# A decoder layer on one core: the MLP's up projection by seven block products instead of eight, its down projection in a part of its own

## The chip, the cores and the metric
The program runs on one core of one Trainium2 chip. Five engines work side by side: PE (TensorE, matrix products into PSUM), DVE (VectorE), ACT (ScalarE), POOL (GpSimd) and SP, which here only issues DMA. The metric is the device time of one execution in microseconds, lower is better. A framework orders the instructions of each engine ahead of time and puts in the semaphore waits that the tiles' memory calls for.

## The reference, cut to what matters
One decoder layer on 1024 tokens of width 1024, in float32: three token mixers, their gated merge, an output projection, cross-attention over a memory of 256 rows, and a feed-forward part (width 2816) with a causal convolution over three tokens. `u` and `v` are the two halves of one up projection.

```python
def conv_gated_ffn(h, w_up, conv_w, conv_b, w_down):
    u, v = jnp.split(h @ w_up, 2, axis=-1)
    u = lax.conv_general_dilated(u, conv_w[:, None, :], window_strides=(1,),
                                 padding=[(CONV_W - 1, 0)],
                                 dimension_numbers=('NWC', 'WIO', 'NWC'),
                                 feature_group_count=D_FF) + conv_b
    return (jax.nn.silu(u) * v) @ w_down
...
        branches = jnp.stack([o_hg, o_da, o_rw], axis=2)
        gate = jax.nn.sigmoid((g_pre + b_gate[l]).astype(jnp.float32)).astype(x.dtype)
        merged = jnp.sum(gate * jnp.einsum('bsnc,ncd->bsnd', branches, w_branch[l]), axis=2)
        x = x + merged @ w_out[l]
        h = rms_norm(x, norm_xa_g[l])
        x = x + memory_cross_attention(h, rms_norm(mem, norm_mem_g[l]), xa_wq[l], xa_wkv[l], xa_wo[l])
        h = rms_norm(x, norm_ffn_g[l])
        x = x + conv_gated_ffn(h, ffn_w_up[l], ffn_conv_w[l], ffn_conv_b[l], ffn_w_down[l])
    return rms_norm(x, final_norm_g)
```

## The kernel before
Every product is made of three: both operands are split into a high part (a cast to fp32r on ACT) and a low part (the rest, subtracted on DVE or POOL), and PE adds high x high, high x low and low x high in PSUM. A weight is loaded by SP into `raw` (512 KB), split into `whi` and `wlo` by `wsplit` (L125-139), and used as the stationary operand, 128x128 at a time, against 512 tokens. `job` (L141-157) computes 128 output channels for 1024 tokens: 8 channel tiles x 2 token halves x 3 = 48 matmuls into the PSUM tile `ps_d`.

The program's stages are, in order: projections and mixers; the merge of the three branches (2, 1, 0), in which `branch` loads a branch's output `oraw`, splits it, and `merge` multiplies it by the branch's weight and gates it with `mth` (DVE L1170 or L1172, POOL L1173, the running sum `acc`); the trunk (output projection, scores and context, three passes of `tokmajor`, with the norm and the transposes of 128 tokens at a time behind the last column quarter); the feed-forward part. Merge 2 is a background stream that fills PE during the mixers and is emptied by `drain` after the loads of branch 1 have been placed.

`ffn` (L1231-1294) goes two channel tiles f at a time. For each f: 48 matmuls for u, the convolution (ACT L1248, L1250, DVE L1251, L1252, ACT L1253 for silu), 48 for v, their product (DVE L1257), its split (ACT L1259, POOL L1260) and the split of 128 rows of the down weight `wdr` (ACT L1265, POOL L1266). Then `down` adds the two tiles' share of the output: 16 groups of 6 matmuls into `ps_dn`, and each group is added to the residual `xr` by DVE (L1290), 11 times over in all. PE alternates between the two products to the end.

The order of the work within an engine is set by the framework's scheduler, which simulates the program; two instructions may be swapped only if no data or memory stands between them. SP issues its loads in its own order: a load that waits for a buffer holds up those behind it. Tiles with one tag in a pool share `bufs` buffers; a pool opened after another is closed takes the same memory, and its first writers wait for the last readers there.

## Time and profile before
| what | value |
|---|---|
| time, median of 3 runs | 2477.51 us (2473.56 to 2480.95) |
| the profiled execution | 2482.2 us, span 2480.3 us, mean granted clock 0.99 |
| instructions | 36628, of these 15488 matmul rows on PE |
| busy: PE, weight loads, DVE, ACT, POOL | 97%, 81%, 47%, 32%, 22% |
| DMA, mean over the span | 80 GB/s |

Matmuls are pipelined: a row gives the duration of one from its start to the modelled end (0.39 us), while the next starts 0.23 us later, so the steps between starts are what a matmul costs. The feed-forward part runs from about 1754 us to the end, the merge from about 1300 to 1440, the trunk between them. A row of a group gives busy time and mean duration; the idle time after the bar is that of the engine before those instructions.

### The profile page before, as it was taken

What the parts mean: (1) busy time and instruction counts of PE and PEld (TensorE: products, weight loads), DVE (VectorE), ACT (ScalarE), POOL (GpSimd) and SP (SyncE); (2) the same over time, 40 slices, a digit from 0 to 9 for tenths busy, and PEclk for the clock granted to TensorE, in tenths of its full rate; (3) what the DMA queues carried; (4) which work ended last, traced back from release to release, by engine and by line L of the source; (5) the groups of instructions that cost most, each with busy time, mean ns of one, the idle gap of its engine ahead of it and who ended that gap; (6) DMA issues with size and microseconds to landing.
All of it is one profiled execution on the core that took longest, in us unless ns stands there. A gap on an engine that the chain in (4) does not pass through costs nothing.

```text
span 2480.3 us, 36628 instructions
## 1 busy us (share of the span) xinstructions
PE 2413.2 (97%) x15488; PEld 2018.9 (81%) x15488; DVE 1161.6 (47%) x1911; ACT 790.9 (32%) x1163; POOL 552.1 (22%) x465
## 2 busy tenths in 40 slices
...
GB/s 299 232 153 128 81 57 94 56 94 40 95 66 65 59 48 35 52 43 52 43 64 205 183 118 57 89 69 35 77 50 36 51 43 43 51 52 51 51 34 68
DMA packets 78436, 199.65 MB, mean 80 GB/s; under 512 B 23616, under 2 KB 28352, under 8 KB 78272
## 3 DMA queue, kind: packets, MB, share of 16 engines
...
## 4 chain that ended last, share of the span: by engine, by line
PE 81%; DVE 9%; issue 3%; ACT 3%; DMA 2%; POOL 2%; SPq 0%; DVEq 0%; POOLq 0%; ACTq 0%
PE ps_d L152 16%; PE ps_d L150 16%; PE ps_d L154 16%; PE ps_dn L1273 10%; PE ps_tm L1089 3%; PE ps_tm L1090 3%; PE ps_tm L1091 3%; PE ps_l L937 1%; PE ps_c L274 1%; DVE tha L450 1%; DVE tmpa L448 1%; PE ps_Y L274 1%; PE ps_o L766 1%; PE ps_T L1135 1%; PE ps_qk L1051 1%
## 5 line engine op out<-in xcount | busy, mean ns | idle before, releaser
L135 ACT CAST whi<-raw 128x1024 fp32r<-128x1024 f32 (+1 forms) x198 | 196.3, 997 | 749.9 <-PE ps_d L152 554.3
L150 PE MATMUL ps_d<-hThi,whi 128*128 128x512 f32 x1056 | 427.5, 405 | 2.6 <-DVE Ktt L256 2.2
L152 PE MATMUL ps_d<-hTlo,whi 128*128 128x512 f32 x1056 | 425.9, 404 | 0.0
L154 PE MATMUL ps_d<-hThi,wlo 128*128 128x512 f32 x1056 | 425.2, 403 | 0.0
L138 POOL TENSOR_TENSOR wlo<-raw,whi 128x1024 fp32r<-128x1024 f32 (+1 forms) x67 | 149.7, 2234 | 731.8 <-ACT whi L135 685.0
L1290 DVE TENSOR_TENSOR xr<-ps_dn,xr 128x512 f32<-128x512 f32 x176 | 119.9, 688 | 344.8 <-PE ps_dn L1273 344.6
L152 PE MATMUL ps_d<-h3Tlo,whi 128*128 128x512 f32 x704 | 275.4, 391 | 0.0
L154 PE MATMUL ps_d<-h3Thi,wlo 128*128 128x512 f32 x704 | 275.3, 391 | 0.0
L150 PE MATMUL ps_d<-h3Thi,whi 128*128 128x512 f32 x704 | 275.1, 391 | 0.1
L1273 PE MATMUL ps_dn<-wdh,ffact 128*128 128x512 f32 x704 | 246.4, 396 | 0.1
L150 PEld LDWEIGHTS ps_d<-hThi,whi 128*128 128x128 f32 x1056 | 200.6, 190 | 45.4 <-issue 3.2
L152 PEld LDWEIGHTS ps_d<-hTlo,whi 128*128 128x128 f32 x1056 | 200.6, 190 | 43.1 <-issue 4.8
L154 PEld LDWEIGHTS ps_d<-hThi,wlo 128*128 128x128 f32 x1056 | 200.4, 190 | 43.1 <-issue 4.2
L138 DVE TENSOR_TENSOR wlo<-raw,whi 128x1024 fp32r<-128x1024 f32 (+1 forms) x131 | 169.4, 1300 | 90.8 <-ACT whi L135 90.7
L1273 PEld LDWEIGHTS ps_dn<-wdh,ffact 128*128 128x128 f32 x704 | 132.2, 188 | 31.3 <-DVE xr L1290 0.5
L152 PEld LDWEIGHTS ps_d<-h3Tlo,whi 128*128 128x128 f32 x704 | 132.2, 188 | 29.6 <-DVE h3Tlo L1139 0.4
L150 PEld LDWEIGHTS ps_d<-h3Thi,whi 128*128 128x128 f32 x704 | 132.0, 188 | 29.5 <-ACT h3Thi L1138 0.3
L154 PEld LDWEIGHTS ps_d<-h3Thi,wlo 128*128 128x128 f32 x704 | 132.2, 188 | 29.2 <-POOL wlo L138 0.2
L1273 PE MATMUL ps_dn<-wdl,ffact 128*128 128x512 f32 x352 | 138.4, 393 | 0.0
L1260 POOL TENSOR_TENSOR ffact<-y,ffact 128x1024 fp32r<-128x1024 f32 (+1 forms) x23 | 57.6, 2505 | 174.2 <-ACT ffact L1259 174.2
L1273 PEld LDWEIGHTS ps_dn<-wdl,ffact 128*128 128x128 f32 x352 | 66.0, 188 | 15.4
L740 DVE CUSTOM_DVE_ANT_0 a_p<-ps_s,a_bias 128x512 f32<-128x512 f32 (+3 forms) x96 | 51.8, 552 | 52.3 <-PE ps_s L738 46.7
...
## 6 DMA issues: line engine op xcount, KB each, us to landing
raw<-t_in SPq DMA_DIRECT2D x66, 512.0 KB, 3.7
raw<-t_up SPq DMA_DIRECT2D x44, 512.0 KB, 3.6
th_dram<-th SPq DMA_DIRECT2D x24, 512.0 KB, 2.9
mth<-th_dram SPq DMA_DIRECT2D x24, 512.0 KB, 3.8
wdr<-ffn_w_down SPq DMA_DIRECT2D x22, 512.0 KB, 3.5
raw<-t_kv SPq DMA_DIRECT2D x16, 512.0 KB, 4.9
raw<-qk_dram SPq DMA_DIRECT2D x16, 512.0 KB, 3.6
oraw<-o_dram SPq DMA_DIRECT2D x12, 512.0 KB, 4.7
```

Source lines behind the costliest of these rows:

```text
L135: nc.scalar.copy(out=hi, in_=raw)
L138: eng.tensor_tensor(out=lo, in0=raw, in1=hi.bitcast(F32), op=ALU.subtract)
L150: nc.tensor.matmul(o, lhsT=hi[:, k, :], rhs=xhi(k, h), start=(k == 0), stop=False)
L152: nc.tensor.matmul(o, lhsT=hi[:, k, :], rhs=xlo(k, h), start=False, stop=False)
L154: nc.tensor.matmul(o, lhsT=lo[:, k, :], rhs=xhi(k, h), start=False, stop=(k == nk - 1))
L740: V.tensor_tensor_reduce(out=p_[:, a:b], in0=ps[:, 0:b - a], in1=bias[:, 1024 - n + a:1024 - n + b], op0=ALU.add, op1=ALU.max, scale=1.0, ...
L1089: nc.tensor.matmul(o, lhsT=xh, rhs=hi[:, k % 4, :], start=(k == 0), stop=False)
L1090: nc.tensor.matmul(o, lhsT=xh, rhs=lo[:, k % 4, :], start=False, stop=False)
L1091: nc.tensor.matmul(o, lhsT=xl, rhs=hi[:, k % 4, :], start=False, stop=(k == NK - 1))
L1260: G.tensor_tensor(out=lo, in0=y[:, ts], in1=hi.bitcast(F32), op=ALU.subtract)
L1273: T.matmul(ps, lhsT=acts[f][a][:, P * i:P * i + P], rhs=wd[f][b][:, 512 * c:512 * c + 512], start=(f == 0 and n == 0), stop=(f == NG - 1 a ...
L1290: V.tensor_tensor(out=xr[i][:, cs], in0=ps, in1=xr[i][:, cs], op=ALU.add)
```

## The change
Three stages are rewritten, and the memory between them is laid out anew.

- Up projection (`left`, `prod`, `right`, `ffn_up`). For each f the weights of u and v (rows of blocks A1, A2) by two halves of the channels, and the normed input by two channel halves and two token halves (B11 to B22), form products of two by two blocks. Seven products of sums of blocks replace the eight: S1 = A21 + A22, S2 = S1 - A11, S3 = A11 - A21, S4 = A12 - S2; T1 = B12 - B11, T2 = B22 - T1, T3 = B22 - B12, T4 = B21 - T2. The sums S are made on POOL (128x512) for each f, each of the seven left operands is split into a form `wf` (ACT, then DVE and POOL in turn). The right operands are made once, in `right`, from raw transposed copies of the normed input (`h3r`, 128x2048). The products are added up in PSUM where two share a target, and else by DVE from PSUM. The first three f start with the products that need no T. The gated product y is stored to DRAM.
- Down projection (`ffn_down`) after all f: for each half of the tokens all 22 tiles of weights and of the stored y are loaded and split, and all eight PSUM banks sum over the 22 tiles; the last three f are held back so that the four token tiles end one after another. The residual is stored in DRAM by the trunk and loaded again.
- Trunk and merge: the context projection runs in two passes of four token tiles (`split=True`); activations lie in 15 buffers of 8 KB a partition instead of 6 of 16 KB; merge 2 is emptied and its pool closed before branch 1 is loaded.

```diff
     def halves(self, nm):
-        return [[self.actp.tile([P, NK, 512], F32R, tag="act", name=f"{nm}{p}{h}") for h in range(2)] for p in ("hi", "lo")]
+        return [[[self.quad(f"{nm}{p}{h}") for g in range(2)] for h in range(2)] for p in ("hi", "lo")]
+
+    def quad(self, nm, dt=F32R, shape=(P, 4, 512)):
+        return self.actp.tile(list(shape), dt, tag="act", name=nm)
...
         self.tokmajor(qk_dram, h2, soft, split=True)
...
+        def last(q, i, o):
+            xs = xr[i][:, 256 * q:256 * q + 256]
+            V.tensor_tensor(out=xs, in0=o, in1=xs, op=ALU.add)
+            if q < 3:
+                return
+            nc.sync.dma_start(out=x2_dram[i], in_=xr[i])
...
+                A.copy(out=raw[g, i // 4][:, :, ts], in_=p3)
+                if i < 4:
+                    hi, lo = (x[:, :, ts] for x in X[g])
+                    A.copy(out=hi, in_=p3)
+                    V.tensor_tensor(out=lo, in0=p3, in1=hi.bitcast(F32), op=ALU.subtract)
+
+        self.tokmajor(vo_dram, pT, last, split=True)
+        return X, raw
...
+    def left(self, r1, r2, which, sp):
...
+        sums = {"S1": ("A21", "A22", ALU.add), "S2": ("S1", "A11", ALU.subtract), "S3": ("A11", "A21", ALU.subtract),
+                "S4": ("A12", "S2", ALU.subtract)}
...
+                G.tensor_tensor(out=q[n], in0=a, in1=b, op=op)
...
+            f = self.wp.tile([P, 2, 4, P], F32R, tag=("whi", "wlo")[self.nform % 2], name="wf")
+            A.copy(out=f[:, 0], in_=x)
+            (V if self.nform % 2 else G).tensor_tensor(out=f[:, 1], in0=x, in1=f[:, 0].bitcast(F32), op=ALU.subtract)
+            yield f
+
+    def prod(self, ps, f, x, start, stop):
+        n = 0
+        for k in range(4):
+            for a, b in ((0, 0), (0, 1), (1, 0)):
+                self.nc.tensor.matmul(ps, lhsT=f[:, a, k, :], rhs=x[b][:, k, :], start=(start and n == 0), stop=(stop and n == 11),
+                                      skip_group_check=not start)
+                n += 1
...
+        b11, b21, b12, b22 = raw[0, 0], raw[1, 0], raw[0, 1], raw[1, 1]
+        V.tensor_tensor(out=b11, in0=b12, in1=b11, op=ALU.subtract)
+        t2 = self.quad("t2r", F32)
+        V.tensor_tensor(out=t2, in0=b22, in1=b11, op=ALU.subtract)
+        G.tensor_tensor(out=b12, in0=b22, in1=b12, op=ALU.subtract)
+        X["T2"] = parts(t2, "T2", V)
+        X["T3"] = parts(b12, "T3", V)
+        G.tensor_tensor(out=b21, in0=b21, in1=t2, op=ALU.subtract)
+        X["T1"] = parts(b11, "T1", V)
+        X["T4"] = parts(b21, "T4", G)
+        X["B22"] = parts(b22, "B22", G)
...
+                vt = self.res.tile([P, S], F32, tag=f"r{6 + f % 2}", name="vt")
...
+                self.prod(b, next(forms), X["T2"], True, True)
+                V.tensor_tensor(out=u2, in0=b, in1=s1, op=ALU.add)
+                self.prod(c, next(forms), X["T3"], True, True)
+                V.tensor_tensor(out=u3, in0=c, in1=u2, op=ALU.add)
+                self.prod(d, next(forms), X["T1"], True, True)
+                V.tensor_tensor(out=vt[:, 512:1024], in0=d, in1=u3, op=ALU.add)
+                if a is not None:
+                    second(a, forms, u[:, 2:514])
+                else:
+                    G.tensor_copy(out=u[:, 2:514], in_=c11)
+                self.prod(c, next(forms), X["T4"], False, True)
+                V.tensor_tensor(out=vt[:, 0:512], in0=c, in1=u2, op=ALU.add)
+                self.prod(d, next(forms), X["B22"], False, True)
+                V.tensor_tensor(out=u[:, 514:1026], in0=d, in1=u2, op=ALU.add)
+                y = self.res.tile([P, S], F32, tag=f"r{f % 2}", name="y")
+                A.activation(out=y, in_=u[:, 2:], func=AF.Identity, scale=col(2, f), bias=col(3, f))
+                V.scalar_tensor_tensor(out=y, in0=u[:, 1:S + 1], scalar=col(1, f), in1=y, op0=ALU.mult, op1=ALU.add)
+                V.scalar_tensor_tensor(out=y, in0=u[:, 0:S], scalar=col(0, f), in1=y, op0=ALU.mult, op1=ALU.add)
+                A.activation(out=y, in_=y, func=AF.Silu)
+                G.tensor_tensor(out=y, in0=y, in1=vt, op=ALU.mult)
+                nc.sync.dma_start(out=act[f], in_=y)
...
+            ne = 3
+            rs = [load(f) for f in range(ne)]
+            fo = [self.left(*r, ("A11", "A12", "S2", "S3", "S1", "A22", "S4"), sp) for r in rs]
+            early = [first(f, fo[f], (self.tps, self.tps, self.mps)[f]) for f in range(ne)]
...
+            self.right(X, raw)
+            for f in range(NFF):
+                if f < ne:
+                    rest(f, fo[f], early[f][1], None, c11[f])
+                    continue
+                forms = self.left(*load(f), ("A11", "S2", "S3", "S1", "A12", "A22", "S4"), sp)
+                a, s1 = first(f, forms, self.tps)
+                rest(f, forms, s1, a, None)
...
+        with tc.tile_pool(name="down", bufs=1) as sp:
...
+                held = []
+                for f in range(NFF):
+                    wr = sp.tile([P, DM], F32, tag="wdr", name="wdr", bufs=2)
+                    nc.sync.dma_start(out=wr, in_=I["ffn_w_down"][0, P * f:P * f + P, :])
+                    w = self.quad("wd", shape=(P, 2, DM))
+                    A.copy(out=w[:, 0], in_=wr)
+                    (V if f % 2 else G).tensor_tensor(out=w[:, 1], in0=wr, in1=w[:, 0].bitcast(F32), op=ALU.subtract)
+                    ar = sp.tile([P, 512], F32, tag="acr", name="acr", bufs=3)
+                    nc.sync.dma_start(out=ar, in_=act[f, :, 512 * tg:512 * tg + 512])
+                    a = self.wp.tile([P, 2, 512], F32R, tag=("whi", "wlo")[f % 2], name="ap")
+                    A.copy(out=a[:, 0], in_=ar)
+                    V.tensor_tensor(out=a[:, 1], in0=ar, in1=a[:, 0].bitcast(F32), op=ALU.subtract)
+                    if f < NFF - tail:
+                        for j in range(4):
+                            step(f, j, (w[:, 0], w[:, 1]), a)
+                    else:
+                        held.append((f, (w[:, 0], w[:, 1]), a))
+                for j in range(4):
+                    i = 4 * tg + j
+                    for f, w, a in held:
+                        step(f, j, w, a)
                     for c in range(2):
                         cs = slice(512 * c, 512 * c + 512)
+                        V.tensor_tensor(out=xr[j][:, cs], in0=ps[j][c], in1=xr[j][:, cs], op=ALU.add)
+                    y = sp.tile([P, DM], F32, tag="fin", name="fin", bufs=2)
+                    self.norm_out(sp, xr[j], g4, y, out[0, P * i:P * i + P, :], i == 7)
 def program(tc, I, O, ctx):
...
     b.attn_mixers(o_dram[1], o_dram[0], lambda n: b.gate_jobs(gp, th, n), tail())
-    b.actp = ctx.enter_context(tc.tile_pool(name="act", bufs=6))
+    b.drain()
+    c3.close()
+    b.actp = ctx.enter_context(tc.tile_pool(name="act", bufs=15))
     with tc.tile_pool(name="mgt", bufs=2) as mg:
-        parts = b.branch(o_dram[1], b.actp, mg)
-        b.drain()
-        for _ in b.merge(1, th, mg, parts):
+        for _ in b.merge(1, th, mg, b.branch(o_dram[1], b.actp, mg)):
             pass
         mT = b.halves("mT")
         for _ in b.merge(0, th, mg, b.branch(o_dram[0], b.actp, mg), mT):
             pass
...
-    b.ffn(h3, xr, O["out"])
+    b.ffn_up(X, raw, act)
+    b.ffn_down(act, x2, O["out"])
```

On SP, where merge 2 gives way to merge 1, before (`oraw` is a branch's output, `raw<-t_br` a weight of the merge, `mth` a gate):

```order
204 L1150 DMA oraw<-o_dram 128x1024 x2
205 L1166 DMA mth<-th_dram 128x1024 x3
206 L132 DMA raw<-t_br 128x512
207 L1150 DMA oraw<-o_dram 128x1024 x2
208 L132 DMA raw<-t_br 128x512
```

and now, from the same load of branch 1:

```order
206 L1175 DMA mth<-th_dram 128x1024
207 L137 DMA raw<-t_br 128x512
208 L1159 DMA oraw<-o_dram 128x1024 x2
209 L1175 DMA mth<-th_dram 128x1024 x2
210 L137 DMA raw<-t_br 128x512
211 L1159 DMA oraw<-o_dram 128x1024 x5
```

The first loads of branch 1 stood before the last two gates of merge 2; now they follow all eight. On DVE at the same place, before (rows 1213, 1214, 1218 and 1222 are the last four `acc` of merge 2):

```order
1213 L1170 SCALAR_TENSOR_TENSOR acc<-mth,ps_d 128x1024
1214 L1170 SCALAR_TENSOR_TENSOR acc<-mth,ps_d 128x1024
1215 L138 TENSOR_TENSOR wlo<-raw,whi 128x512
1216 L1152 TENSOR_TENSOR act<-oraw,act 128x1024
1217 L1152 TENSOR_TENSOR act<-oraw,act 128x1024
1218 L1170 SCALAR_TENSOR_TENSOR acc<-mth,ps_d 128x1024
1219 L1152 TENSOR_TENSOR act<-oraw,act 128x1024
1220 L138 TENSOR_TENSOR wlo<-raw,whi 128x512
1221 L1152 TENSOR_TENSOR act<-oraw,act 128x1024
1222 L1170 SCALAR_TENSOR_TENSOR acc<-mth,ps_d 128x1024
```

and now:

```order
1213 L1179 SCALAR_TENSOR_TENSOR acc<-mth,ps_d 128x1024
1214 L1179 SCALAR_TENSOR_TENSOR acc<-mth,ps_d 128x1024
1215 L143 TENSOR_TENSOR wlo<-raw,whi 128x512
1216 L1179 SCALAR_TENSOR_TENSOR acc<-mth,ps_d 128x1024
1217 L1179 SCALAR_TENSOR_TENSOR acc<-mth,ps_d 128x1024
1218 L143 TENSOR_TENSOR wlo<-raw,whi 128x512
1219 L1161 TENSOR_TENSOR olo<-oraw,ohi 128x1024
```

The low parts of branch 1 (`act<-oraw` before, `olo` now) stood between the last sums of merge 2; now all sums come first. On POOL, at the passage from the trunk to the feed-forward part, before (the last norms, then the first weights' low parts):

```order
318 L1104 TENSOR_SCALAR ms<-ms 128x1
319 L1105 TENSOR_TENSOR rs<-ms,mhalf 128x1
322 L1247 MEMSET u 128x2
323 L1266 TENSOR_TENSOR wdl<-wdr,wdh 128x1024
324 L138 TENSOR_TENSOR wlo<-raw,whi 128x1024
325 L1266 TENSOR_TENSOR wdl<-wdr,wdh 128x1024
```

and now (`S` are sums of weight blocks, `h3r` the raw quarters that become T3 and T4, `wf` a form's low part):

```order
325 L1280 TENSOR_TENSOR S_15747<-S_15745,raw 128x512
326 L1313 TENSOR_TENSOR h3r_15439<-h3r_15446,h3r_15439 128x2048
327 L1316 TENSOR_TENSOR h3r_14886<-h3r_14886,t2r 128x2048
328 L1280 TENSOR_TENSOR S_15747<-raw,S_15747 128x512
329 L1369 COPY u<-c_15662 128x512
330 L1288 TENSOR_TENSOR wf<-S_15765,wf 128x512
331 L1280 TENSOR_TENSOR S_15847<-raw 128x512
332 L1288 TENSOR_TENSOR wf<-raw,wf 128x512
333 L1307 TENSOR_TENSOR T4lo<-h3r_14886,T4hi 128x2048
334 L1280 TENSOR_TENSOR S_15867<-raw 128x512
335 L1280 TENSOR_TENSOR S_15849<-S_15847,raw 128x512
336 L1307 TENSOR_TENSOR B22lo<-h3r_15446,B22hi 128x2048
```

Four operations on 128x2048 stand among the weight forms that the first products need.

## Rows read from the trace of the kernel before

**Rows 1.** The page's head: busy time, share of the span, instructions.
```profile
PE 2413.2 (97%) x15488; PEld 2018.9 (81%) x15488; DVE 1161.6 (47%) x1911; ACT 790.9 (32%) x1163; POOL 552.1 (22%) x465
```

**Rows 2.** The chain of waits by line, shares of the span.
```profile
PE ps_d L152 16%; PE ps_d L150 16%; PE ps_d L154 16%; PE ps_dn L1273 10%; PE ps_tm L1089 3%; PE ps_tm L1090 3%; PE ps_tm L1091 3%; PE ps_l L937 1%; PE ps_c L274 1%; DVE tha L450 1%; DVE tmpa L448 1%; PE ps_Y L274 1%; PE ps_o L766 1%; PE ps_T L1135 1%; PE ps_qk L1051 1%
```

**Rows 3.** Windows: stretch and us, busy per engine, PE clock, DMA share, GB/s.
```profile
1800.00:1900.00 100.00, 100.00 (x436) 81.49 (x435) 32.69 (x38) 20.82 (x20) 20.00 (x11) 1.00 0.13 43
```

**Rows 4.** Timeline of PE, merge 2 to merge 1: start, duration, instruction.
```profile
1349.62 0.39 PE L154 MATMUL ps_d<-ohi,wlo 128*128 128x512 f32 x1
1349.85 0.39 PE L150 MATMUL ps_d<-act,whi 128*128 128x512 f32 x1
...
1358.01 0.39 PE L150 MATMUL ps_d<-act,whi 128*128 128x512 f32 x1
```

**Rows 5.** Timeline of PE near the end of the down projection.
```profile
2468.86 0.40 PE L1273 MATMUL ps_dn<-wdl,ffact 128*128 128x512 f32 x1
...
2472.36 0.39 PE L1273 MATMUL ps_dn<-wdl,ffact 128*128 128x512 f32 x1
```

**Rows 6.** Groups, 1800 to 2400 us, shapes apart: busy, mean ns, idle before.
```profile
L1290 DVE TENSOR_TENSOR xr<-ps_dn,xr 128x512 f32<-128x512 f32 x144 | 98.4, 689 | 305.6 <-PE ps_dn L1273 305.6
...
L1260 POOL TENSOR_TENSOR ffact<-y,ffact 128x1024 fp32r<-128x1024 f32 x18 | 47.8, 2656 | 142.4 <-ACT ffact L1259 142.4
...
L1266 POOL TENSOR_TENSOR wdl<-wdr,wdh 128x1024 fp32r<-128x1024 f32 x18 | 43.5, 2415 | 67.9 <-ACT wdh L1265 67.9
...
L138 DVE TENSOR_TENSOR wlo<-raw,whi 128x1024 fp32r<-128x1024 f32 x18 | 28.0, 1555 | 0.0
L1251 DVE SCALAR_TENSOR_TENSOR y<-u,par,y 128x1024 f32<-128x1024 f32 x18 | 24.4, 1355 | 29.3 <-ACT y L1250 25.8 <-POOL wlo L138 3.6
...
L1252 DVE SCALAR_TENSOR_TENSOR y<-u,par,y 128x1024 f32<-128x1024 f32 x18 | 22.9, 1270 | 0.0
L1257 DVE TENSOR_TENSOR y<-y,ps_d 128x1024 f32<-128x1024 f32 x18 | 22.0, 1222 | 71.7 <-PE ps_d L154 71.7
```

**Rows 7.** Timeline of SP, DVE and ACT around merge 1's start.
```profile
1336.50 0.79 SPq L1150 DMA_DIRECT2D oraw<-o_dram  x2
...
1347.52 1.22 DVE L1170 SCALAR_TENSOR_TENSOR acc<-mth,ps_d 128x1024 f32<-128x1024 f32 x1 [1.52 <-DMA mth<-th_dram]
...
1349.48 1.05 ACT L1151 CAST act<-oraw 128x1024 fp32r<-128x1024 f32 x1 [4.22 <-DMA oraw<-o_dram]
1350.43 0.62 ACT L135 CAST whi<-raw 128x512 fp32r<-128x512 f32 x1
```

**Rows 8.** DMA issues: count, KB each, median us from issue to landing.
```profile
wdr<-ffn_w_down SPq DMA_DIRECT2D x22, 512.0 KB, 3.5
...
oraw<-o_dram SPq DMA_DIRECT2D x12, 512.0 KB, 4.7
```

**Rows 9.** Windows of 5 us, columns as in rows 3, PE's first.
```profile
1240.00:1245.00 5.00, 5.00 (x18) 4.02 (x17) 3.02 (x9) 0.64 (x3) 0.22 (x1) 0.66 0.02 3
...
1225.00:1230.00 5.00, 3.95 (x21) 2.95 (x20) 4.04 (x8) 5.00 (x8) 5.00 (x5) 1.00 0.00 0
...
1750.00:1755.00 5.00, 3.96 (x24) 2.67 (x23) 2.91 (x5) 2.25 (x4) 0.10 (x1) 1.00 0.00 0
```

**Rows 10.** Timeline of PE in the attention mixer, idle time in brackets.
```profile
1228.85 0.66 PE L761 MATMUL ps_at<-ident,a_p 128*128 128x128 f32 x4 [0.84 <-DVE a_p L755]
...
1239.51 0.50 PE L737 MATMUL ps_s<-a_k,a_q 128*128 128x512 f32 x1 [2.46 <-DVE a_mx L740]
```

**Rows 11.** The tile `mth`: duration ns min/median/max, first and last start, landing.
```profile
L1173 POOL TENSOR_TENSOR acc<-acc,mth x16: 2379/2776/3392, 1359.2 to 1440.0; 128x1024 f32<-128x1024 f32 x16
...
DMA to landing us min/median/max: 3.2/3.8/8.4
```

**Rows 12.** Groups on POOL over the span, shapes apart.
```profile
L915 POOL TENSOR_TENSOR h_M<-h_b 128x512 f32<-128x512 f32 x28 | 33.2, 1184 | 69.8 <-PE ps_l L927 46.9 <-issue 8.5 <-ACT a_vT L781 6.1
...
L138 POOL TENSOR_TENSOR wlo<-raw,whi 128x512 fp32r<-128x512 f32 x12 | 17.5, 1461 | 55.1 <-ACT whi L135 55.1
```

More of the change, by code (lines that the diff above doesn't have):

```diff
@@ L89, in shape_consts, with blk @@
     return c
+def blk(t, g):
+    return t[g] if isinstance(t, list) else t[:, 4 * g:4 * g + 4, :]
 class K:
@@ L1087, in tokmajor @@
                     hi, lo = w[k // 4]
-                    xh, xl = xt[0][i // 4][:, k, ts], xt[1][i // 4][:, k, ts]
+                    xh, xl = (blk(xt[a][i // 4], k // 4)[:, k % 4, ts] for a in range(2))
                     nc.tensor.matmul(o, lhsT=xh, rhs=hi[:, k % 4, :], start=(k == 0), stop=False)
@@ L1136, in to_T @@
             p3 = ps.rearrange("p (k t) -> p k t", t=P)
-            hi, lo = (T2[a][i // 4][:, 4 * g:4 * g + 4, ts] for a in range(2))
+            hi, lo = (blk(T2[a][i // 4], g)[:, :, ts] for a in range(2))
             nc.scalar.copy(out=hi, in_=p3)
@@ L1220, in soft @@
             ts = slice(P * (i % 4), P * (i % 4) + P)
-            hi, lo = (pT[a][i // 4][:, 2 * q:2 * q + 2, ts] for a in range(2))
+            hi, lo = (blk(pT[a][i // 4], q // 2)[:, 2 * (q % 2):2 * (q % 2) + 2, ts] for a in range(2))
             A.copy(out=hi, in_=p3)
@@ new lines, in prod, with right, parts @@
+    def prod(self, ps, f, x, start, stop):
[5 more added lines that the diff above has]
+                n += 1
+    def right(self, X, raw):
+        nc = self.nc
+        V, A, G = nc.vector, nc.scalar, nc.gpsimd
+        def parts(x, nm, eng):
+            f = [self.quad(f"{nm}{p}") for p in ("hi", "lo")]
+            A.copy(out=f[0], in_=x)
+            eng.tensor_tensor(out=f[1], in0=x, in1=f[0].bitcast(F32), op=ALU.subtract)
+            return f
+        b11, b21, b12, b22 = raw[0, 0], raw[1, 0], raw[0, 1], raw[1, 1]
[9 more added lines that the diff above has]
+        X["B22"] = parts(b22, "B22", G)
```

181 lines of the change are left out of this document (102 added, 79 removed).

## The prediction, on record before the changed kernel ran
> **What bounds the kernel now.** I read the page's head first: TensorE's matmuls are busy for 2413.2 of 2480.3 us, and VectorE, next among the others, for less than half [rows 1]. Then the chain of waits: the reader is to see the two products of the feed-forward part, `ps_d` and `ps_dn`, lead its lines [rows 2]. Then the windows: between 1800 and 2400 us, where the up and down projections alternate, 100 us hold 436 matmuls, PE is never idle, its clock is 1.00, and DVE, ACT and POOL are busy for a third, a fifth and a fifth [rows 3]. So this part is paid per matmul: fewer matmuls pay at once as long as nothing else comes late, and any new wait of PE adds in full.
>
> **What goes.** Up projection: 2 x 22 tiles x 48 = 2112 matmuls of 512 columns before; after, 22 x 7 products x 12 (four channel tiles, three hi/lo terms) = 1848. That is 264 fewer. From 1349.62 to 1358.01 us, 37 steps, a `ps_d` matmul starts every 0.227 us [rows 4]; the mixed stretch has 0.229 [rows 3]. 264 x 0.227 = **-59.9 us**. The down projection keeps its 1056 matmuls, at 0.233 us (15 steps from 2468.86 to 2472.36) [rows 5]; if summing over all channels moved them to 0.227, that is -6.3 us; if they slowed as much, +6.3. I take 0. 160 of the 176 DVE additions of 0.69 us go [rows 6]; they waited for PE, and PE has no idle time there [rows 3]: 0.
>
> **(a) Branch 1 of the merge: a new wait of PE.** Before, the first two `oraw` loads are issued at 1336.50 us, and merge 1's first matmul starts at 1349.85, one step behind merge 2's last [rows 4, 7]. Now merge 2 is drained and its pool closed first. The order shows all eight `acc` of DVE ahead of the first `olo`, and the first load writes memory that merge 2's tiles held, so it must wait for the last `acc`. After the last matmul: `acc` 1.22, landing 4.7, cast 1.05, and `olo` like `acc` 1.22 [rows 7, 8]: 8.2 to the second matmul. There are two raw buffers, so the loads of k=2 and 3 wait for a used one: some 2 more. **+10** (8 to 13). On SP two `mth` loads stand behind the waiting one; they are needed only at merge 1's first eviction.
>
> **(c) Up to down: a second one.** Before, both alternate. Now the first `wdr` load writes where `u` stood, so it waits for the last convolution term. From the last up matmul: DVE sum 0.69, ACT 1.05, two DVE terms 1.36 + 1.27, landing 3.5, ACT cast 1.05, POOL's low part 2.42, before which only the first matmul of the product can start [rows 6 to 8]. Sum 11.3; **+11** (8 to 13). On SP the store of the last `y` and the next loads stand behind it; they come later than this chain only if the landing is shared.
>
> **Clock, in both.** After PE stood idle for 2.46 us before 1239.51, its clock was 0.66 over 1240 to 1245: (1 - 0.66) / 0.5 x 5 = 3.4 us at the lower level (1.2 GHz), half of it lost: 1.7 us. An idle 0.84 before 1228.85 left it at 1.00 [rows 9, 10]. Both new gaps are longer than 2.46: **+1.7 each**.
>
> **(b) Into the up part.** The four raw quarters of the normed input become T1 to T4 by sums and splits of 128x2048; four of these stand in POOL's queue between the weight forms. POOL took a median of 2.78 us for a 1024-wide sum and 2.42 for a 1024-wide low part [rows 6, 11], so 5 us each (4.8 by twice the quickest sum, 6.8 by twice the slowest). The early products give PE 48 matmuls, 11 us, as cover after the last transposes; behind it I estimate from these prices waits of 1.5 (T1 after T2), 2.5 (T3), 1.6 (T4's low part), 2.1 (B22's) and 2 for POOL's backlog in the next two f, 9.7 in all. The 1.04 us that PE stood idle there before, at 1750 to 1755 [rows 9], goes: **+8** after rounding down (4 to 16; the low end if DVE's share comes early, the upper if each POOL operation is waited for).
>
> **(e) Up part, steady.** Per f, 84 matmuls = 19.1 us on PE. POOL: four sums at 1.18, 3.5 low parts of 512 at 1.46, `y*vt` 2.66 = 12.5; DVE 5 sums and 3.5 low parts at 0.69, and 2.63 = 8.5; ACT 7 casts and 2 copies at 0.62, and 2.1 = 7.7 [rows 6, 7, 12]. No engine is full, but there is one chain: from the last product with B22, DVE sum 0.69, ACT 1.05, two DVE terms with a sum between them 3.3, silu 1.05, the copy to `u` 0.62, the cast of an S2 form 0.62, the last three in that order on ACT: 7.3, and 8.4 to 8.8 with DVE's low parts and semaphore steps between. The next product with that form follows 33 to 35 matmuls later, 7.5 to 7.9 us. So 0.5 to 0.9 late every second f, little in the others, and some 0.2 where a sum in PSUM waits for its reader: 0.55 a f over 20 f, **+11** (2 to 22: 0.1 and 1.1 a f).
>
> **(d) Rest.** The context projection loads and splits its weights twice, 8 more of 512 KB, and has fewer buffers: **+1** (0 to 5). Down part: 24 matmuls = 5.6 us per f against 768 KB, 140 GB/s, where a pair of `wdr` has a cycle of 3.5 + 1.05 + 2.42 = 7.0 of 11.2 us [rows 6 to 8]: 0.
>
> At one place the Trainium skill would change the sum. Row first: a low part of 1024 with both inputs in SBUF took DVE 1.56 us beside POOL, a product of 1024 with one input in PSUM 1.22 [rows 6]. "GPSIMD Engine Reference", section 1 (Specifications), says that POOL's SBUF interfaces are shared with VectorE, with contention when a DVE instruction has two SBUF inputs; the rows agree by 0.3 us. By it the terms (b) and (e) would grow, towards the second rival.
>
> **Sum.** -59.9 + 10 + 11 + 3.4 + 8 + 11 + 1 = -15.5. The profiled execution took 2482.2 us, 4.7 above the median of the three runs, 2477.5. 2482.2 - 15.5 - 4.7 = **2462 us**, 0.6% faster; a measurement here tells about 0.3% (7.4 us) from no change.
>
> **Rivals.**
> - Clean: only the two gaps cost, and (b), (d), (e) are hidden. For it: no helper is above 66% of an f. Against: four POOL operations of 5 us in one queue. -59.9 + 11.7 + 12.7 = -35.5: 2442. Chance 0.24.
> - Slower: the helpers set the pace of the up part. One mechanism: the chain of (e), whose links lengthen when DVE and POOL run beside each other (a POOL sum spreads from 2.38 to 3.39 us [rows 11]; DVE's low part 1.56 against 1.22). Break-even is at (59.9 - 11.7 - 12.7 - 9) / 20 = 1.3 us a f. A chain of 9.9 us against 7.7 costs 2.2 a f, +44 in place of +11: 2495. Against: the chain's own rows add up to 7.3. Chance 0.10.
> - The down part is bound by its loads: landings at the slow end of a 512 KB load (8.4 instead of 3.8 [rows 11]) make 11.9 us per pair against 11.2, and `acr` comes behind; 0.7 to 2 us per pair x 22 = +15 to +44, about 2485. Against: 43 GB/s are moved there now [rows 3], so queues are empty. Chance 0.05.
> - Many short waits let the clock fall: each of some 20 waits of (e) would lose 1.7 us more, +34: 2496. Against: the 0.84 us wait left it at 1.00 [rows 9, 10]. Chance 0.03. That is the rule of the Trainium skill, "TensorE: Matmul & The Clock Gate", in "A second HAM failure mode: psum-queue depth-cycling": frequent short idles between groups of matmuls make the clock swing between its levels. The row speaks against it for a single wait; no run here shows a train of them.
> - It does not do what it says: then PE's matmul rows would not fall by 264. The order shows products of 12 and 1056 down matmuls, so 0.
>
> **How the numbers follow.** Forecast 0.58, rivals 0.24, 0.10, 0.05, 0.03. The forecast's own range, with its bounds seldom all at one end: 2450 to 2478. With most of the clean case and the near side of the slower ones, 8 in 10: 2440 to 2486. Faster by over 0.3% (under 2470): the clean case and three quarters of the forecast, 0.67. Within 0.3% (2470 to 2485): the rest of the forecast and half of the load-bound case, 0.18. Slower: 0.15.
>
> **What would show it.** Right: 264 fewer matmuls; PE idle for 8 to 13 us between merge 2's last matmul and merge 1's first ones, ended by ACT or DVE behind an `oraw` landing; the same before the first `ps_dn` matmuls, ended by the low part of `wd`; a lower clock behind each; idle PE in the up part in pieces below 1 us, ended by `wf`. Wrong: windows of the up part with PE under 93% busy (second rival), clock under 1.00 there (fourth), `ps_dn` waiting for DMA (third), or no idle PE between trunk and up (first).

## The result: 0.5% slower, and the profile after

The changed kernel took 2491.22 us (median of 6, 2485.53 to 2492.26), the kernel before 2476.69 beside it; the ratio is 1.0054, 95% interval 1.004 to 1.0069. Predicted were 2462 us, 80% range 2440 to 2486. The profiled execution has a span of 2490.5 us against 2480.3, so 10.2 us more are to be found there.

The page's head of the changed kernel, as [rows 1]:

```profile
PE 2368.3 (95%) x15224; PEld 1973.5 (79%) x15224; DVE 1245.7 (50%) x1964; ACT 885.6 (36%) x1359; POOL 760.4 (31%) x614
```

264 matmuls are gone, as counted. PE's busy time fell by 45 us, and the span rose: PE stands idle for 55 us more. Windows of 40 us of the changed kernel, columns as in [rows 3], show where:

```profile
1320.00:1360.00 40.00, 34.27 (x146) 27.38 (x145) 14.10 (x14) 6.83 (x10) 5.09 (x5) 0.91 0.59 206
1760.00:1800.00 40.00, 26.14 (x90) 19.79 (x90) 30.24 (x12) 16.98 (x20) 39.84 (x15) 0.80 0.10 27
1800.00:1840.00 40.00, 34.39 (x138) 26.92 (x137) 21.54 (x20) 13.12 (x17) 28.91 (x23) 0.94 0.20 66
1920.00:1960.00 40.00, 39.67 (x173) 31.85 (x172) 17.95 (x21) 14.94 (x22) 27.38 (x21) 1.00 0.25 80
2200.00:2240.00 40.00, 28.12 (x113) 22.12 (x112) 17.61 (x17) 12.93 (x16) 11.98 (x8) 0.87 0.54 191
2320.00:2360.00 40.00, 31.52 (x119) 24.02 (x118) 16.35 (x16) 13.35 (x18) 12.65 (x7) 0.83 0.55 176
```

Four places: the merge, the passage from trunk to up (POOL busy for 39.84 of 40 us, DMA at a share of 0.10), up to down, and one that no step of the prediction had, in the middle of the down part. Each has a lower clock. Between them, at 1920, PE is all but full. PE's timeline of the changed kernel has the longest waits, in brackets, with what ended each (`<-DVE T2lo` is DVE's low part of T2, `u` its sums, `ap` the split of the stored y on ACT):

```profile
1353.19 1.22 PE L155 MATMUL ps_d<-ohi,whi 128*128 128x512 f32 x2 [5.70 <-DMA oraw<-o_dram]
...
1779.80 0.79 PE L1295 MATMUL ps_b<-T2lo,wf 128*128 128x512 f32 x1 [8.12 <-DVE T2lo L1307]
...
1791.03 0.60 PE L1295 MATMUL ps_cd<-T1hi,wf 128*128 128x512 f32 x1 [3.19 <-DVE u L1363]
...
1814.66 0.47 PE L1295 MATMUL ps_cd<-T1hi,wf 128*128 128x512 f32 x1 [4.02 <-DVE u L1363]
...
2226.69 107.26 PE L1423 MATMUL ps_dn<-wd,ap 128*128 128x512 f32 x462 [10.08 <-ACT ap L1436]
...
2338.37 1.22 PE L1423 MATMUL ps_dn<-wd,ap 128*128 128x512 f32 x2 [4.42 <-ACT ap L1436]
...
2345.29 1.22 PE L1423 MATMUL ps_dn<-wd,ap 128*128 128x512 f32 x2 [3.41 <-ACT ap L1436]
```

Why the passage is so long is seen when POOL and DVE of the changed kernel are laid side by side (start, duration):

```profile
1768.07 4.60 POOL L1313 TENSOR_TENSOR h3r<-h3r,h3r 128x2048 f32<-128x2048 f32 x1
1772.63 4.97 POOL L1316 TENSOR_TENSOR h3r<-h3r,t2r 128x2048 f32<-128x2048 f32 x1
1777.54 3.35 POOL L1280 TENSOR_TENSOR S<-raw,S 128x512 f32<-128x512 f32 x1
...
1768.79 4.43 DVE L1288 TENSOR_TENSOR wf<-S,wf 128x512 fp32r<-128x512 f32 x1 [1.84 <-ACT wf L1287]
1773.14 6.61 DVE L1307 TENSOR_TENSOR T2lo<-t2r,T2hi 128x2048 fp32r<-128x2048 f32 x1
...
1794.64 1.30 POOL L1280 TENSOR_TENSOR S<-raw 128x512 f32<-128x512 f32 x1
...
1795.62 0.69 DVE L1365 TENSOR_TENSOR vt<-ps_cd,u 128x512 f32<-128x512 f32 x1 [4.74 <-PE ps_cd L1295]
```

A low part of 512 that DVE does in 0.69 us lasts 4.43, to just past the end of POOL's 4.60. T2's low part starts 0.5 us after POOL's next operation and ends 2.2 us after it; POOL's 512-wide sum, 1.30 at 1794.64, then lasts 3.35, of which 2.2 lie beside T2's. So it reads as if the two did not run at the same time but one after the other. The DVE sum with an operand in PSUM at 1795.62 keeps its 0.69 beside POOL.

These are not picked cases. From 1760 us on, 36 of DVE's 512-wide operations with both inputs in SBUF began more than 0.15 us before a running POOL operation ended, and each ended 0.55 us after it. Of 75 with an operand in PSUM that began so, none took more than 0.69 us. The runs below test what this costs.

### The profile page after: what moved, and what is told of

The parts are those of the page before. It is cut to its first block, busy times and chain, and to the rows that moved or that the text cites. A ratio compares the mean times of both kernels' runs of the same rounds, so it can differ in the third digit from the quotient of the medians.

```text
span 2490.5 us, 36955 instructions
## 1 busy us (share of the span) xinstructions
PE 2368.3 (95%) x15224; PEld 1973.5 (79%) x15224; DVE 1245.7 (50%) x1964; ACT 885.6 (36%) x1359; POOL 760.4 (31%) x614
## 3 DMA queue, kind: packets, MB, share of 16 engines
q1 hardware_dynamic: 93248, 241.47, 29.5%
## 5 line engine op out<-in xcount | busy, mean ns | idle before, releaser
L1423 PE MATMUL ps_dn<-wd,ap 128*128 128x512 f32 x1056 | 247.0, 396 | 18.6 <-ACT ap L1436 17.9
L1423 PEld LDWEIGHTS ps_dn<-wd,ap 128*128 128x128 f32 x1056 | 201.6, 192 | 63.9 <-ACT ap L1436 19.5
L143 POOL TENSOR_TENSOR wlo<-raw,whi 128x1024 fp32r<-128x1024 f32 (+1 forms) x45 | 96.0, 2133 | 448.7 <-ACT whi L140 354.2
L1295 PE MATMUL ps_a<-h3hi,wf 128*128 128x512 f32 x352 | 116.1, 393 | 2.4 <-ACT wf L1287 0.7
L1287 ACT CAST wf<-S 128x512 fp32r<-128x512 f32 x88 | 54.6, 623 | 128.1 <-PE ps_cd L1295 79.2
L1432 POOL TENSOR_TENSOR wd<-wdr,wd 128x1024 fp32r<-128x1024 f32 x22 | 53.2, 2418 | 108.4 <-ACT wd L1431 108.4
L155 PE MATMUL ps_d<-ohi,whi 128*128 128x512 f32 x192 | 75.6, 397 | 7.1 <-DMA oraw<-o_dram 5.7
L1295 PEld LDWEIGHTS ps_a<-h3hi,wf 128*128 128x128 f32 x352 | 66.0, 188 | 20.3 <-ACT wf L1287 5.5
L1288 POOL TENSOR_TENSOR wf<-S,wf 128x512 fp32r<-128x512 f32 x43 | 62.2, 1447 | 61.4 <-ACT wf L1287 61.3
L1094 PE MATMUL ps_tm<-whi,h2Thi 128*128 128x256 f32 x256 | 75.3, 294 | 1.7 <-ACT s_p L1222 1.7
```

The source lines that it names most:

```text
L143: eng.tensor_tensor(out=lo, in0=raw, in1=hi.bitcast(F32), op=ALU.subtract)
L155: nc.tensor.matmul(o, lhsT=hi[:, k, :], rhs=xhi(k, h), start=(k == 0), stop=False)
L1094: nc.tensor.matmul(o, lhsT=xh, rhs=hi[:, k % 4, :], start=(k == 0), stop=False)
L1287: A.copy(out=f[:, 0], in_=x)
L1288: (V if self.nform % 2 else G).tensor_tensor(out=f[:, 1], in0=x, in1=f[:, 0].bitcast(F32), op=ALU.subtract)
L1295: self.nc.tensor.matmul(ps, lhsT=f[:, a, k, :], rhs=x[b][:, k, :], start=(start and n == 0), stop=(stop and n == 11), skip_group_check=not ...
```

## The experiments

Times are compared with the changed kernel's 2491.2 us unless a text names another; with each kernel the kernel before ran on the same chip. Its median was 2476.7 us beside the changed kernel, 2476.6 beside the first four runs (DVE, acr, early loads, raw buffers) and 2474.6 to 2474.8 beside all others. So the gains of those others read about 2 us too large; where it matters, the gain against the kernel before stands in brackets. Stage lengths below are taken from the profiled execution of each run.

**right() on DVE.** POOL's four operations of 128x2048 are moved.

```diff
-        G.tensor_tensor(out=b12, in0=b22, in1=b12, op=ALU.subtract)
+        V.tensor_tensor(out=b12, in0=b22, in1=b12, op=ALU.subtract)
...
-        X["T4"] = parts(b21, "T4", G)
-        X["B22"] = parts(b22, "B22", G)
+        X["T4"] = parts(b21, "T4", V)
+        X["B22"] = parts(b22, "B22", V)
```

> Compared with the changed kernel (2491.2 us); the four 128x2048 operations of right() that stood on POOL are on DVE. Theory (shared port: an operation of DVE with two SBUF inputs and one of POOL do not run at the same time, they wait for each other): T2's low part, 6.61 us there, falls to under 3.5 us because no long POOL operation is beside it, the 8.1 us wait of PE before the second product falls below 5 us, and the kernel is 8 to 14 us faster, since 4 x 4.7 us of POOL become 4 x 2.3 us of DVE in one serial queue. Rival (no sharing; 6.6 us is what DVE pays for a 2048-wide low part, and the stage is bound by DVE's own queue): T2's low part stays at 6 to 7 us and four more of 3 to 6.6 us on DVE make the passage longer, 5 to 20 us slower.

Measured: 2480.94 us, 10.3 faster, though DVE has four long operations more. DVE and POOL in this run:

```profile
1768.52 2.28 DVE L1316 TENSOR_TENSOR h3r<-h3r,t2r 128x2048 f32<-128x2048 f32 x1
1770.73 2.69 DVE L1307 TENSOR_TENSOR T2lo<-t2r,T2hi 128x2048 fp32r<-128x2048 f32 x1
...
1771.25 3.31 POOL L1280 TENSOR_TENSOR S<-raw,S 128x512 f32<-128x512 f32 x1
```

T2's low part takes 2.69, PE's wait for it 1.80 instead of 8.12. A 2048-wide operation is 2.28 us on DVE against 4.6 to 5.0 on POOL. The theory holds in time and rows; its rival would have made the kernel slower. DVE's queue is now what is left to wait for: a later sum on it keeps PE waiting for 6.13 us.

```profile
1773.47 0.80 PE L1295 MATMUL ps_b<-T2lo,wf 128*128 128x512 f32 x1 [1.80 <-DVE T2lo L1307]
...
1787.38 0.77 PE L1295 MATMUL ps_cd<-T1hi,wf 128*128 128x512 f32 x1 [6.13 <-DVE u L1363]
```

**acr from ACT's queue.** In the down part `wdr` is a loaded weight and `wd` its split, `acr` is the stored y loaded again and `ap` its split. `nc.sync.dma_start(out=ar, ...)` becomes `nc.scalar.dma_start(out=ar, ...)`.

> The loads of the stored y (acr) are issued from ACT's queue instead of SP's. Theory (in SP's order two wdr loads stand before each acr, so the first token half of the down projection gets one acr per pair of wdr, 7.2 us, against 5.5 us of PE per f; the lead of the first loads is eaten up by about 2338 us): the idle of 4.4 and 3.4 us before 2338 and 2345 us and the lower clock behind it go, 11 to 16 us faster. Rival (the down part is bound by what DMA delivers, 768 KB per f, or by the three held tiles at the half's end): the idle time stays or moves, within 4 us of the changed kernel.

Measured: 2490.67 us, no gain; the waits in the middle are 3.76 and 3.53 us. My theory falls in the form it had: SP's order alone is not what holds `ap`. ACT's timeline in the changed kernel shows another queue with the same pattern:

```profile
2327.32 1.05 ACT L1431 CAST wd<-wdr 128x1024 fp32r<-128x1024 f32 x1 [4.62 <-DMA wdr<-ffn_w_down]
2328.62 1.05 ACT L1431 CAST wd<-wdr 128x1024 fp32r<-128x1024 f32 x1 [0.24 <-DMA wdr<-ffn_w_down]
2329.57 0.61 ACT L1436 CAST ap<-acr 128x512 fp32r<-128x512 f32 x1
2334.60 1.04 ACT L1431 CAST wd<-wdr 128x1024 fp32r<-128x1024 f32 x1 [4.41 <-DMA wdr<-ffn_w_down]
```

Two casts of `wd` stand before most casts of `ap`, and wait for their loads. SP issues such a pair of loads every 7.1 to 8.3 us from 2285 us on, and an `ap` comes every 6.6 us on average, where PE uses one in 24 x 0.227 = 5.4. With 15 buffers the weights of the second half are fetched in the first; the lead of the first loads is used up near the half's end.

**Six buffers for the split down weights.** This run tells that from a bound by the four buffers of `ap`.

```diff
             tail = 3
+            wds = [self.quad("wd", shape=(P, 2, DM)) for _ in range(6)]
...
-                    w = self.quad("wd", shape=(P, 2, DM))
+                    w = wds[(NFF * tg + f) % 6]
```

> The split down weights have 6 buffers instead of a ring of 15, so that they can't run far ahead of the stored y. Theory (ACT's queue holds two casts of wd for each cast of ap, and each waits for its load, so that ap comes every 7 us or more in the first token half): the waits of 4.4 and 3.4 us near 2338 and 2345 us go, with the low clock behind them, 10 to 15 us faster than the changed kernel's 2491.2. Rival (the end of the half is gated by the four buffers of ap and the three held tiles, whatever the weights do): the waits stay, less than 4 us.

Measured: 2476.06 us, 15.2 faster (13.3 against the kernel before), where 10 to 15 were expected. The waits in the middle are gone, and ACT alternates one to one, `ap` now waiting for PE:

```profile
2308.79 0.62 ACT L1437 CAST ap<-acr 128x512 fp32r<-128x512 f32 x1 [3.87 <-PE ps_dn L1424]
2309.31 1.05 ACT L1432 CAST wd<-wdr 128x1024 fp32r<-128x1024 f32 x1
2314.23 0.62 ACT L1437 CAST ap<-acr 128x512 fp32r<-128x512 f32 x1 [3.87 <-PE ps_dn L1424]
```

**Early loads of the down part.** `wdr` goes into residual buffers in the first half, `acr` into the weights' raw buffers in both.

```diff
-                    wr = sp.tile([P, DM], F32, tag="wdr", name="wdr", bufs=2)
+                    wr = self.res.tile([P, DM], F32, tag=f"r{4 + f % 2}", name="wdr") if tg == 0 else sp.tile([P, DM], F32, tag="wdr", name="wdr", bufs=2)
...
-                    ar = sp.tile([P, 512], F32, tag="acr", name="acr", bufs=3)
+                    ar = self.wp.tile([P, 512], F32, tag="raw", name="acr")
```

> In the first half of the down projection wdr is loaded into two residual buffers that are free by then and acr into the weights' raw buffers, so neither waits for the last convolution term. Theory (the gap between up and down is that chain: sum, convolution, landing, cast): the 10.1 us of idle time before the first down product fall below 2 us, and the lower clock behind it goes, 10 to 13 us faster, as far as the acr order at the end of the half does not take it back. Rival (PE would wait there anyway, for PSUM banks or for the last y): the gap stays above 6 us.

Measured: 2471.53 us, 19.7 faster, well above the 10 to 13 expected. PE's waits of this run from 2195 to 2360 us:

```profile
2209.09 4.15 PE L1423 MATMUL ps_dn<-wd,ap 128*128 128x512 f32 x17 [0.69 <-DVE ap L1437]
...
2227.79 132.57 PE L1423 MATMUL ps_dn<-wd,ap 128*128 128x512 f32 x577 [6.05 <-ACT ap L1436]
```

10.08 became 0.69, and the first down products now stand between the last up products. The waits in the middle gave way to one of 6.05 right behind the last up product, where a cast of `ap` again follows two of `wd`. So the gain holds part of what six buffers give, which the forecast had not counted.

**Branch 1 into the weights' raw buffers.** `b.branch(o_dram[1], b.actp, mg)` becomes `b.branch(o_dram[1], b.actp, b.wp)`.

> Branch 1 (and 0 stays as it is) is loaded into the weights' raw buffers instead of the merge's new pool, so its first loads no longer wait for the last sum of merge 2; the casts' target still does. Theory (the gap at merge 1 is landing after the last sum): the 5.7 us of idle time before merge 1's first product fall to 2 to 3.5 us, the clock dips less or not, 4 to 7 us faster. Rival (the gap is set by the casts' target and by the weights that now share those buffers): less than 2 us faster, or slower.

Measured: 2497.78 us, 6.6 slower. The wait is 17.24 us now, ended by a weight:

```profile
1359.15 0.80 PE L155 MATMUL ps_d<-ohi,whi 128*128 128x512 f32 x1 [17.24 <-ACT whi L140]
```

SP issues four `oraw` from 1344.05 us and merge 1's first weight, which shares their buffers, only at 1355.87. The rival holds.

**Branch 1 before merge 2 is emptied.** 13 of the 15 activation buffers (`act`) are opened first, with a raw pool of their own; two more (`act2`) after it.

```diff
-    b.drain()
+    b.actp = ctx.enter_context(tc.tile_pool(name="act", bufs=13))
+    with tc.tile_pool(name="mgr", bufs=2) as mgr:
+        parts = b.branch(o_dram[1], b.actp, mgr)
+        b.drain()
     c3.close()
-    b.actp = ctx.enter_context(tc.tile_pool(name="act", bufs=15))
+    b.act2 = ctx.enter_context(tc.tile_pool(name="act2", bufs=2))
...
-        X["T4"] = parts(b21, "T4", G)
         X["B22"] = parts(b22, "B22", G)
+        X["T4"] = parts(b21, "T4", G)
```

> Branch 1 is loaded before merge 2 is emptied again: 13 of the 15 activation buffers are opened ahead of it with a raw pool of its own, the other two after it (they hold the parts of B22, which are made before T4's). Theory (merge 1's start waits for memory that merge 2 holds): the 5.7 us of idle time and the clock's dip behind it go, 8 to 11 us faster than 2491.2. Rival (its weights, or the gates' loads in SP's queue, take the place of the wait): less than 4 us faster.

Measured: 2477.62 us, 13.6 faster (11.7 against the kernel before), where 8 to 11 were expected. The window of the merge in this run:

```profile
1330.00:1360.00 30.00, 30.00 (x134) 24.83 (x133) 13.52 (x13) 9.22 (x11) 5.95 (x5) 1.00 0.79 275
```

No idle time and no dip: the wait was for memory that merge 2 held. From merge 2's last matmul to the trunk's first it is 87.7 us instead of 98.5, so 10.8 come from there, inside the forecast. The rest is no gain of the passage: from the trunk's last matmul to the last up product this run, which also has the new order of B22 and T4, is 3.6 us longer (468.8 against 465.2). The down part is 4.6 shorter, with 2.35 and 1.73 us for the largest waits in its middle; why was not tested. And 3.4 lie ahead of the merge, where the two kernels are the same.

**The sums T in the trunk.** For token tiles 4 to 7, on pieces of 128x4x128:

```diff
+            V.tensor_tensor(out=t1, in0=pp[0], in1=b11, op=ALU.subtract)
+            V.tensor_tensor(out=t2, in0=pp[1], in1=t1, op=ALU.subtract)
+            V.tensor_tensor(out=t3, in0=pp[1], in1=c12, op=ALU.subtract)
+            for nm, x in (("B22", pp[1]), ("T2", t2), ("T3", t3), ("T1", t1)):
+                hi, lo = (q[:, :, ts] for q in X[nm])
+                A.copy(out=hi, in_=x)
+                V.tensor_tensor(out=lo, in0=x, in1=hi.bitcast(F32), op=ALU.subtract)
+            V.tensor_tensor(out=b21, in0=b21, in1=t2, op=ALU.subtract)
```

(`pp` are the transposes in PSUM, `c12` ACT's copy of the first.)

> The sums T1, T2, T3 and the parts of T1, T2, T3 and B22 are made for 128 tokens at a time in the trunk's last pass, on DVE and ACT, with an operand in PSUM where there is one; of T4 only the split is left for the end, on DVE. Theory (the passage was bound by DVE and POOL working one at a time on operands in SBUF, some 48 us of work in one queue from 1760 us): the passage's work behind the last transposes falls by more than half, its loss of about 28 us by 14 to 24 us, so 2467 to 2477. Rival (the weight forms on POOL and their sums are the bound there): less than 10 us faster.

Measured: 2478.86 us, 12.4 faster (10.5 against the kernel before): less than the theory's 14 to 24, and hardly more than the rival's 10. The 8.12 us wait is gone, but DVE is now busy for 29.5 of the 31 us from 1745 to 1776, and the transposes wait for the PSUM tiles that it reads, 4.43 and 2.77 us. So the largest waits left at the passage are for DVE.

**Together.** Three edits (right() on DVE, early loads, six buffers):

> The edits of three runs together: right() on DVE, the early loads of the down projection, and six buffers of split down weights. If the three causes are separate, their gains add: 10 (measured) + 10 to 20 + what six buffers give, less what the early loads have already taken: 2452 to 2464 us, faster than the kernel before by over 0.4%. If the second half of the early loads' gain was the same wait that six buffers remove, it comes out at 2459 to 2464.

Measured: 2456.64 us. The sum of the single gains, 45.2, came to 34.6: the last two share a wait. It lies in the first range, 2.4 us below the second.

With branch 1 early besides:

> The edits of four runs together: right() on DVE, early loads of the down projection, six buffers of split down weights, branch 1 loaded before merge 2 is emptied. If the gap at merge 1 is a wait of its own, e7's 13.6 us add to e6's 2456.6: 2441 to 2446 us. If e7's gain came in part from the new order of B22 and T4 at the end of right() (which DVE does here), it comes out at 2446 to 2452.

Measured: 2447.25 us, in the second range: 9.4 of the 13.6 us add. The reason is not the one given for it. Stage by stage, the merge gives 11.1 us, about what it gave alone, and up to the last up product the run is 3.2 us longer, as it was alone (3.6). What does not add is the 4.6 of the down part: with six buffers its middle has no waits left to lose. The new order is a cost: B22's low part stands before T2's on DVE, and PE waits for T2's 6.15 us, where the run without the early branch has 1.79.

```profile
1755.03 2.28 DVE L1307 TENSOR_TENSOR B22lo<-h3r,B22hi 128x2048 fp32r<-128x2048 f32 x1
...
1761.53 3.35 DVE L1307 TENSOR_TENSOR T2lo<-t2r,T2hi 128x2048 fp32r<-128x2048 f32 x1
...
1764.93 0.80 PE L1295 MATMUL ps_b<-T2lo,wf 128*128 128x512 f32 x1 [6.15 <-DVE T2lo L1307]
```

With the sums T in the trunk instead of right() on DVE:

> As the last, with the sums T1 to T3 made for 128 tokens at a time in the trunk's last pass (as in e8) in place of right() on DVE. e8 was 2 us faster than e1 alone: 2438 to 2444 us if that holds here too; if the transposes that wait for DVE in e8 (4.4 and 2.8 us) cost as much as it saves, the same as the last run within 3 us.

Measured: 2437.61 us, 9.6 better than the last run, ratio to the kernel before 0.985 (0.9836 to 0.9865). This version beats both kernels. Alone, the same edit was only 2 us ahead of right() on DVE. It gives more here since it also takes away what the new order had cost the last run: from the trunk's last matmul to the last up product it is 462.2 us against 468.3 there, 6.1 less. Another 2.7 us lie ahead of the merge, where the two kernels are the same.

**Eight products, the rest as changed.** `ffn_up` is the old pair of `dense_m` per f with the store of y; the trunk makes high and low parts of all four quarters.

```diff
+                pu = self.dense_m(I["t_up"][f], hhi, hlo, late=(f == 0))
...
+                pv = self.dense_m(I["t_up"][NFF + f], hhi, hlo, late=(f == 0))
+                V.tensor_tensor(out=y, in0=y, in1=pv, op=ALU.mult)
+                nc.sync.dma_start(out=act[f], in_=y)
```

> The changed kernel with one part undone: the up projection is eight products again (48 matmuls a tile, convolution, product and store of y as before, right operands without sums), while the down projection in its own part, the memory's new order and the emptied merge stay. Theory (the new waits at merge 1, at the start of the down part and at its middle cost 10.9 + 12.6 + 14.3 us by the trace, and the down part's faster steps give 7 back; the seven products themselves gain 60 and lose some 28 at the passage and 9 in steady state): slower than the changed kernel, 2500 to 2514 us. Rival (the seven products cost more than they save): faster than the changed kernel, under 2488.

Measured: 2494.99 us: 3.8 above the changed kernel (5.9 against the kernel before), as the theory's sign had it, but 5 below its range. One of its terms was wrong: there is no wait between up and down in this run, so that gap belongs to the seven products' memory and not to the separate down part. Its other waits are those of the changed kernel (5.71 us at the merge, 4.10 and 3.71 in the middle). The whole stretch is at the quick step, 442 matmuls in 100 us, where [rows 3] has 436:

```profile
1800.00:1900.00 100.00, 100.00 (x442) 82.81 (x442) 23.11 (x18) 24.86 (x24) 12.49 (x10) 1.00 0.20 69
```

**Eight products with the repairs** (early loads, six buffers, early branch 1):

> Eight products as in the last run, with the early loads of the down projection, its six buffers and the early branch 1. What is left of the change then is the down projection in a part of its own, whose matmuls follow each other in 0.227 instead of 0.233 us. Theory: 5 to 10 us faster than the kernel before, 2465 to 2472. Rival (the faster step belongs to something else, or the stores and loads of y take it back): 2473 to 2480.

Measured: 2472.39 us, ratio 0.9991 (0.998 to 1.0002): 2.2 us faster, not to be told from none, at the edge between the two cases. A new wait of 3.06 us at the last transposes takes some of it. It ends with DVE's low part of the tile before, which follows ACT's cast, and that cast stands behind early casts of down weights:

```profile
1751.35 1.04 ACT L1294 CAST wd<-wdr 128x1024 fp32r<-128x1024 f32 x1 [1.53 <-DMA wdr<-ffn_w_down]
1752.30 1.07 ACT L1143 CAST h3Thi<-ps_T 128x512 fp32r<-128x512 f32 x2
...
1754.31 1.25 PE L1140 MATMUL ps_T<-ident,xn 128*128 128x128 f32 x8 [3.06 <-DVE h3Tlo L1144]
```

Against this run's 2472.39 the seven products give 25 us (2447.25) or 35 (2437.61) of the 60.

## Why the prediction was wrong, step by step

The steps in the profiled execution, worked out from windows and matmul steps:

| step | predicted us | measured us |
|---|---|---|
| 264 matmuls | -59.9 | -59.9 (count as predicted) |
| (a) merge 1, with clock | +11.7 | +10.9 |
| (b) into the up part | +8 | +31 |
| (e) steady up part | +11 | +11 |
| (c) up to down, with clock | +12.7 | +12.6 |
| middle of the down part | 0 | +13 |
| step of the down matmuls | 0 (bounds 6.3 either way) | -7 |
| (d) and the rest, by difference to 10.2 | +1 | -2 |

(a) is the growth of the distance from merge 2's last matmul to the trunk's first. Its sum came out by two misses that cancel: 7.6 us of idle time where 10 had been forecast, and 3.3 for the clock behind it where 1.7 had. For (b) and (e): from 1760.2 to 2216.5 us 1824 up matmuls take 456.3 us, 42.6 above 0.2268 each (0.227 before rounding). The steady loss is read from one instruction per f, silu on ACT in the changed kernel:

```profile
1951.69 1.07 ACT L1378 ACTIVATE y<-y 128x1024 f32<-128x1024 f32 x1 [2.81 <-DVE y L1377]
1971.01 1.06 ACT L1378 ACTIVATE y<-y 128x1024 f32<-128x1024 f32 x1 [2.48 <-DVE y L1377]
1990.95 1.07 ACT L1378 ACTIVATE y<-y 128x1024 f32<-128x1024 f32 x1 [2.81 <-DVE y L1377]
```

19.32 and 19.94 us in turn, 19.63 on average, against 84 x 0.227 = 19.07: 0.56 late. The prediction had 0.55, with every second f late. The size is right, the pattern is not: by PE's own steps each f loses, 0.5 and 0.6 us in turn, in a few longer steps around the place where the next `wf` comes, with 0.1 and 0.2 us of idle time ended by it. Over 20 f that is 11; the rest, 31, is the passage. Of these 31, 20.6 us are idle time of PE from 1760 to 1860 us and some 9 are matmuls at the lower clock behind it (granted on average 0.90 there, 1.00 from 1860 to 2200). The down part: 265.5 us from the last up matmul's start to the last matmul's, 239.5 for 1056 steps of 0.2268; of the 26.0 between, 12.6 are the first gap (10.2 idle, 2.4 by the clock) and 13.4 the middle (8.5 idle, 4.9 by the clock). Windows of the changed kernel give the step and the clock:

```profile
1355.00:1360.00 5.00, 5.00 (x18) 3.97 (x17) 0.56 (x1) 0.17 (x1) 0.00 (x0) 0.73 1.02 407
2225.00:2230.00 5.00, 3.31 (x8) 2.63 (x9) 2.43 (x1) 2.17 (x3) 2.36 (x1) 0.50 1.00 293
2340.00:2345.00 5.00, 1.88 (x4) 0.97 (x4) 0.25 (x1) 2.37 (x3) 2.12 (x1) 0.50 0.68 233
2360.00:2480.00 120.00, 120.00 (x531) 99.13 (x530) 39.03 (x41) 27.93 (x41) 17.18 (x15) 1.00 0.28 95
```

In the first three, windows of 5 us beside the idle times, the granted clock is 0.50 to 0.73, the lower level for all or part of the window ([rows 9] has 0.66); in the last, without idle time, it is 1.00. Summed over the four places, the clock cost, by this estimate, some 20 us (3.3 + 9 + 2.4 + 4.9); the prediction had 3.4 for it, at two places.

**The step that failed is (b)**, +8 where the runs show +31: the waits were sized as if DVE and POOL worked beside each other at the prices of [rows 6, 11]. The single prices were right (4.6 to 5.0 us for POOL's 2048), but DVE's work came on top: T2's low part, for which (b) has no term, stood behind 9.6 us of POOL, and PE waited 8.12 us for it. Waits of 9.7 us were priced, 20.6 were measured. Besides, (b) has no term for the clock behind its waits, though (a) and (c) have one; that is the 9 us more. The prediction had the row that told it, 1.56 against 1.22 in [rows 6], and the rule of the Trainium skill, "GPSIMD Engine Reference", section 1 (Specifications), that POOL and VectorE share their SBUF interfaces, and left both at "would grow". Another page of the Trainium skill states it in full: "SBUF — State Buffer", section "Who interferes with whom", says that a DVE instruction with two SBUF inputs contends with a POOL instruction that reads SBUF, that this contention is an exclusive lock in which the order of issue decides who blocks, and that at most one SBUF input, outside the 2-port modes, is free of it. The trace agrees in all three (4.43 us for 0.69, ending 0.55 after POOL's 4.60; 0.69 beside POOL with one input in PSUM). With such a lock the two queues add up; an estimate from this case's rows: from 1760 us five operations of DVE at 2.3 us and four of POOL at 4.8 are 30.7, and the weights' sums and low parts for the first f come on top, against 11 us of cover. That is at least 19.7, over the bound of 16 that was given. It is near the second rival, but at the passage: in steady state, where that rival put it, the loss was the 11 us of (e).

**The second is the sentence that priced the down part at 0**, by a cycle of 7.0 us for two f. The cycle was about right (7.1 to 8.3); but in the order of ACT's queue it mostly served one f, since the other `wd` was one of the next half. That order is fixed before the run. The third rival named the place and gave a wrong reason: DMA is not the bound, since the run with six buffers has the same loads and no wait.

Two smaller misses go the other way. The down matmuls' 0.233 us fell to 0.227, at the outer bound that was given. And the up matmuls, 0.229 on average in the mixed stretch before, step at 0.227 now, which gives some 4 us that the prediction left out; in the table they are in the last row. The run with eight products steps at 0.227 throughout its up part too, so the slower steps before go with the alternation of the two products in one stretch; what in it costs them was not tried. The clock rival did not come true: all of steady up runs at 1.00. But its waits there are of 0.1 to 0.2 us of idle time, shorter than that rival had them.

The repairs turn each into what it was worth: early loads and six buffers 19.7 and 15.2 us, which overlap, early branch 1 up to 13.6, DVE for POOL 10.3. With the sums T in the trunk in place of the last, the change is worth 37 us (2437.6 against 2474.6). That this is close to the 35.5 of the prediction's clean rival is chance: the rival left the gaps of (a) and (c) in and took nothing for the passage, while here the gaps are gone and the passage still costs.
